# Eleven of the 22 up steps as seven block products, with their weight sums on GpSimd

## The chip, the cores and the metric

The kernel runs on one core of a Trainium2 chip. The core has five engines that work side by side, each through its own queue in order: TensorE (PE, matrix products; its weight loads are listed as PEld), VectorE (DVE), ScalarE (ACT), GpSimd (POOL) and SyncE (SP), which issues most transfers. Matrix products read SBUF and write PSUM. The metric is the device time of one execution in microseconds (us).

## The reference

One layer of a hybrid backbone over 512 latent tokens of 1024 channels. The change touches its last part alone, a gated feed-forward layer with a convolution of width 3 along the tokens:

```python
def conv_ffn(h, w_up, conv_w, conv_b, w_down):
    u = dwconv_centred(h @ w_up, conv_w, conv_b)
    a, b = u[..., :D_FF], u[..., D_FF:]
    return (jax.nn.silu(a) * b) @ w_down
...
x = x + gt2 * conv_ffn(modulate(x, norm2_g[l], sh2, sc2), w_up[l], ffn_conv_w[l],
                       ffn_conv_b[l], w_down[l])
```

`h` is 512 x 1024, `w_up` 1024 x 5632 (`D_FF` is 2816), `w_down` 2816 x 1024. All numbers are float32.

## The kernel before

**Products.** Each float32 operand is split in two: a high part, cast to the rounded type that PE takes (`S.copy`, L183, on ACT), and a low part, what is left (`V.tensor_tensor`, L184, on DVE). A product is then three matmuls, high by high, high by low and low by high (`gemm`, L238, L239, L241). A weight tile of 128 x 1024 floats is loaded by SP (L177) into one of three buffers `wraw`, and its parts `whi` and `wlo` have two buffers each. `run` issues the load and the split of a weight one key ahead of its use.

**The up projection** is 22 steps, `up_step(t)`. A step makes 128 channels of `a` and 128 of `b` for all 512 tokens: two products of eight blocks of 128 input channels each, 2 x 8 x 3 = 48 matmuls of 512 columns. The input is held as `h2h` and `h2l` (the tiles `mh` and `ml`). From PSUM, `conv` makes one pass on ACT (L2051) and two on DVE (L2052, L2053); ACT applies silu (L2059), and DVE multiplies the halves into `F["x"]` (tile `fx`, L2065). Step 0 is apart: it goes by halves of the tokens as the norm hands them out (`norm2_k`, L2014 to L2021).

**The down projection** (`down_step`, L2302 to L2304) already uses seven block products instead of eight. `f_sums(t)` makes its operand sums from `fx` after each up step: splits into `fs` (L2031 on ACT, L2032 on DVE) and differences (L2040 to L2045).

**Beside the up steps** stand eight of the 32 steps `m_step` of a modulation vector (two passes of DVE over a raw weight, L813), woven among steps 0 to 17; transposes of the residual stream (`x1_turn`, DVE L2113, and four small transfers on SP each); and two `fold`s, chains of transfers that POOL issues (L789 to L793).

**Order.** A scheduler orders each engine's instructions when the program is built, except inside `tc.manual_schedule(engines=...)`, where the named engines take them as written, and for single instructions given to `tc.keep_in_program_order`. An engine then works its queue in that order; a wait at its head holds up all behind it.

## Time and profile before

Three runs took 1214.69, 1215.36 and 1216.09 us. The parts of the profiled execution that matter here:

| what | us |
|---|---|
| median of the runs | 1215.36 |
| the profiled execution's own time | 1215.35 |
| its span, from the first to the last instruction | 1213.6 |
| up steps 1 to 21, from 874.34 to 1102.61 | 228.27 |
| DVE, ACT and POOL busy in these | 163.37, 94.78, 14.14 |
| median from issue to landing of an up weight (512 KB) in that stage | 3.8 |

A group's row names line, engine, operation, the tiles written and read, their shapes and the count, then the total and the mean time (us, ns), then the idle time of the engine just before them and what ended it. A timeline's row starts with the start and the length in us; neighbours of one kind are merged into one row with their count. PE's matmuls overlap, so their rate is read from their starts.

### The profile page before, as it was taken

Reading aid. Unit: us, or ns where it says so; the run is one execution under the profiler, and the core shown is the slowest. Engines: PE = TensorE matmul, PEld = TensorE weight load, DVE = VectorE, ACT = ScalarE, POOL = GpSimd, SP = SyncE. Lnnn points to the kernel's source line nnn. Section 1 sums busy time; section 2 is a strip of 40 time slices with the busy share of each in tenths; the row PEclk is TensorE's granted clock in tenths of the full one; section 3 lists DMA queues with packets and bytes.
Section 4 is the critical chain, followed back from the end, with each engine's and each line's share of the span. In section 5 each row is a group of like instructions: output and inputs, shape, how many; then the busy total and the mean of one; then the engine's idle time right before and its main releaser. Section 6 shows DMA issues by size and latency. Waiting matters only on the chain.

```text
span 1213.6 us, 17847 instructions
## 1 busy us (share of the span) xinstructions
PE 1203.6 (99%) x6429; PEld 1005.6 (83%) x6429; DVE 918.6 (76%) x1476; ACT 684.4 (56%) x1269; POOL 263.8 (22%) x274
## 2 busy tenths in 40 slices
PE   9999999999999999999999999999999999999998
PEld 6798888888878878788787887888988888888886
DVE  4857887888565588788887978677677767668787
ACT  4557887778543467476575664223544343436654
POOL 0000121100102546264382762000200100110021
PEclk9999999999999999999999999999999999999999
DMA  9655889844747737566477668687266634437662
GB/s 367 253 148 185 161 229 271 170 133 139 170 140 240 228 113 199 157 162 192 145 178 264 176 228 265 221 251 242 50 163 148 195 117 138 130 107 226 213 185 97
DMA packets 129417, 224.30 MB, mean 185 GB/s; under 512 B 27336, under 2 KB 70640, under 8 KB 129328
## 3 DMA queue, kind: packets, MB, share of 16 engines
q1 hardware_dynamic: 115248, 195.61, 52.0%
q0 software_dynamic: 13792, 27.27, 10.1%
q8 instruction: 51, 0.84, 0.3%
q14 instruction: 38, 0.31, 0.1%
q10 hardware_dynamic: 288, 0.27, 0.1%
HBM read 196.17 MB, written 45.02 MB: 199 GB/s over the span
## 4 chain that ended last, share of the span: by engine, by line
PE 90%; DMA 3%; DVE 2%; POOL 2%; issue 1%; ACT 1%; SPq 0%; DVEq 0%; POOLq 0%; ACTq 0%
PE acc L241 18%; PE acc L238 18%; PE acc L239 18%; PE score L979 3%; PE po L1028 3%; PE pt L1015 2%; PE mis L582 2%; PE mis L1754 2%; PE mis L1597 2%; PE mis L2304 2%; PE mis L2302 2%; PE mis L2303 2%; DMA xs_d<-xb 1%; PE acc L2304 1%; PE acc L2302 1%
## 5 line engine op out<-in xcount | busy, mean ns | idle before, releaser
L184 DVE TENSOR_TENSOR wlo<-wraw,whi 128x1024 fp32r<-128x1024 f32 (+1 forms) x115 | 148.3, 1289 | 89.2 <-ACT whi L183 88.3
L183 ACT CAST whi<-wraw 128x1024 fp32r<-128x1024 f32 (+1 forms) x115 | 120.2, 1046 | 154.2 <-PE acc L239 103.4
L238 PE MATMUL acc<-hlh,whi 128*128 128x512 f32 x472 | 192.8, 409 | 0.0
L241 PE MATMUL acc<-hlh,wlo 128*128 128x512 f32 x472 | 185.6, 393 | 0.0
L239 PE MATMUL acc<-hll,whi 128*128 128x512 f32 x472 | 185.0, 392 | 0.0
L238 PE MATMUL acc<-mh,whi 128*128 128x512 f32 x368 | 143.3, 389 | 0.0
L239 PE MATMUL acc<-ml,whi 128*128 128x512 f32 x368 | 143.2, 389 | 0.0
L241 PE MATMUL acc<-mh,wlo 128*128 128x512 f32 x368 | 143.2, 389 | 0.0
L241 PEld LDWEIGHTS acc<-hlh,wlo 128*128 128x128 f32 x472 | 88.6, 188 | 19.9 <-issue 0.5
L238 PEld LDWEIGHTS acc<-hlh,whi 128*128 128x128 f32 x472 | 88.8, 188 | 17.6 <-issue 2.8
L239 PEld LDWEIGHTS acc<-hll,whi 128*128 128x128 f32 x472 | 88.9, 188 | 17.4 <-issue 2.2
L238 PEld LDWEIGHTS acc<-mh,whi 128*128 128x128 f32 x368 | 69.1, 188 | 14.4
L241 PEld LDWEIGHTS acc<-mh,wlo 128*128 128x128 f32 x368 | 69.1, 188 | 14.3
L239 PEld LDWEIGHTS acc<-ml,whi 128*128 128x128 f32 x368 | 69.1, 188 | 14.2
L164 POOL DMA_DIRECT2D dsum<-wdn x24 | 25.3, 1118 | 194.3 <-DVE wlo L1112 183.7
L988 DVE CUSTOM_DVE_ANT_0 p<-score,winm,nsink 128x512 f32<-128x512 f32 (+1 forms) x64 | 51.8, 810 | 15.3 <-PE score L979 13.8
L995 ACT ACTIVATE p<-p,mneg 128x512 f32<-128x512 f32 (+1 forms) x64 | 49.7, 777 | 15.4 <-DVE mneg L988 14.9
L813 DVE SCALAR_TENSOR_TENSOR tm<-wraw,csil,tm 128x512 f32<-128x512 f32 x56 | 45.9, 819 | 13.1 <-DMA wraw<-wm 12.4
L1023 DVE TENSOR_TENSOR ptl<-pt,pth 128x512 fp32r<-128x512 f32 x72 | 47.5, 685 | 8.4 <-ACT pth L1019 7.7
L238 PE MATMUL acc<-hch,whi 128*128 128x256 f32 x176 | 53.2, 302 | 0.0
L1112 DVE TENSOR_TENSOR wlo<-wraw,whi 128x1024 fp32r<-128x1024 f32 x30 | 36.7, 1223 | 18.3 <-ACT whi L1109 18.2
L241 PE MATMUL acc<-hch,wlo 128*128 128x256 f32 x176 | 49.8, 283 | 0.0
(458 smaller groups left out, 3054.3 us busy)
## 6 DMA issues: line engine op xcount, KB each, us to landing
wraw<-wup SPq DMA_DIRECT2D x44, 512.0 KB, 4.0
dsum<-wdn POOLq DMA_DIRECT2D x24, 704.0 KB, 8.7
wraw<-wm SPq DMA_DIRECT2D x32, 512.0 KB, 4.1
fb<-cs_d SPq DMA_DIRECT2D x32, 512.0 KB, 7.5
wraw<-wx SPq DMA_DIRECT2D x24, 512.0 KB, 4.1
wm<-wm SPq DMA_DIRECT2D x16, 512.0 KB, 7.9
wraw<-wz SPq DMA_DIRECT2D x16, 512.0 KB, 4.7
far<-us_d SPq DMA_DIRECT2D x32, 256.0 KB, 5.1
```

Of the source, the lines that this page charges most:

```text
L183: F["cast"] = S.copy(hi[:, :n], r[:, :n])
L184: F["sub"] = V.tensor_tensor(lo[:, :n], r[:, :n], raw(hi[:, :n]), ALU.subtract)
L238: T.matmul(ps, wh, xh[:, k0 + k, :], start=a, stop=False)
L239: T.matmul(ps, wh, xl[:, k0 + k, :], start=False, stop=False)
L241: T.matmul(ps, wl, xh[:, k0 + k, :], start=False, stop=b)
L813: V.scalar_tensor_tensor(acc, r[:, u * 512 : u * 512 + 512], sc, acc, ALU.mult, ALU.add)
L988: V.tensor_tensor_reduce(p[:, :w], d["ps"][i][:, o0 : o0 + w], m, op0=ALU.add, op1=ALU.min, scale=1.0, scalar=nsink[:, h : h + 1], accum_o ...
L995: S.activation(p, p, AF.Exp, bias=d["mneg"][:, i : i + 1], scale=-1.0, accum_out=d["den"][:, i : i + 1])
L1023: V.tensor_tensor(d["ptl"][x], d["pt"][x], raw(d["pth"][x]), ALU.subtract)
L1112: sum_step(V.tensor_tensor(d["w"][1], d["r"], raw(d["w"][0]), ALU.subtract), 1 + (4 <= g < 12))
L2302: T.matmul(ps, h, wh, start=st, stop=False, skip_group_check=True)
L2304: T.matmul(ps, h, wl, start=False, stop=en, skip_group_check=True)
```

## The change

Steps 3 to 13 no longer make two whole products. The step's two weight tiles and the input are cut in a 2 x 2 scheme (halves of the input channels, `a` against `b`, halves of the tokens), and seven products of four blocks by 256 columns give what eight would. Weight sums are made by POOL, their casts by ACT and low parts by DVE, all for step t + 1 while PE does step t. The products 7 and 4 of a step run during the next one. The core of it:

```diff
+    def input_sums():
+        r = F["h2"]
+        for e, k in ((G, slice(0, HK, 2)), (V, slice(HK, KT, 2))):
+            tc.keep_in_program_order(e.tensor_tensor(r[:, k, :], raw(h2h[:, k, :]), raw(h2l[:, k, :]), ALU.add))
+        b11, b12, b21, b22 = (r[:, HK * i : HK * i + HK, z] for i in range(2) for z in HALF)
+        for x, y, o in ((b12, b11, b11), (b22, b12, b12), (b22, b11, b22), (b21, b22, b21)):
+            G.tensor_tensor(o, x, y, ALU.subtract)
...
+        if which == 1:
+            G.tensor_tensor(o, wb[:, h[0]], wb[:, h[1]], ALU.add)
+        elif which == 2:
+            G.tensor_tensor(o, B["r1", t], wa[:, h[0]], ALU.subtract)
+        elif which == 3:
+            G.tensor_tensor(o, wa[:, h[0]], wb[:, h[0]], ALU.subtract)
+        else:
+            G.tensor_tensor(o, wa[:, h[1]], B["r2", t], ALU.subtract)
...
+            with tc.manual_schedule(engines=EVERY):
+                if old:
+                    quarter(a, 12)
+                seven(t, 5)
+                if older:
+                    conv_rest("b", b, NFF + b)
+                if new:
+                    seven_sum(n, 1)
+                if old:
+                    conv_first("a", a, a, "tb")
+                kept_half(t, 0, B["y", t])
+                if new:
+                    whole_cast(n)
+                if old:
+                    conv_rest("a", a, a)
+                seven(t, 1)
...
+                seven(t, 3)
...
+                if old:
+                    seven(a, 4)
+                    quarter(a, 21)
+                    conv_first("b", a, NFF + a, "tm")
...
+                seven(t, 6)
...
-            weave([up_step(t) for t in range(18)], msteps[24:]) + [up_step(t) for t in range(18, NFF)],
-            [([], lambda: None)] * 6 + [x1_turn(c) for c in range(8)] + [x1_rows] + [([], lambda: None)] * 6 + [([], row_tiles)],
+            [up_step(t) for t in range(15, 18)],
+            msteps[24:28] + [([], lambda: f_sums(0, 2, True)), ([], lambda: f_sums(2, 4, True))] + msteps[28:] + [x1_rows],
+        )
+        + weave(
+            [up_step(t) for t in range(18, NFF)],
+            [([], lambda p=p: f_sums(p, min(p + 2, DK))) for p in (4, 6, 8, 10)] + [([], row_tiles)],
```

Here `seven(t, j)` is product j of step t on PE, `seven_low` and `whole_low` are DVE's low parts, `seven_cast` and `whole_cast` ACT's casts, `quarter` the adds of partial results from PSUM, `conv_first` and `conv_rest` the convolution, now from SBUF, and `put_up` the product into `fx`, now on POOL. Steps 0 to 2 and 15 to 21 stay as before, and step 14 also makes the last two products of step 13. `f_sums` takes two pairs of steps at once and starts after step 14; for its first two calls POOL takes part of the sums. The modulation's steps 24 to 31 move beside steps 15 to 17.

On DVE, one old step in the middle of the stage (`wlo` and `whi` are parts of a weight, `acc` is PSUM, `ta` and `tc` the two halves after the convolution, `fx` and `fs` belong to the down projection):

```order
L184 TENSOR_TENSOR wlo<-wraw,whi 128x1024
L2052 SCALAR_TENSOR_TENSOR ta<-acc,vec,ta 128x511
L2053 SCALAR_TENSOR_TENSOR ta<-acc,vec,ta 128x511
L184 TENSOR_TENSOR wlo<-wraw,whi 128x1024
L2052 SCALAR_TENSOR_TENSOR tc<-acc,vec,tc 128x511
L2053 SCALAR_TENSOR_TENSOR tc<-acc,vec,tc 128x511
L2065 TENSOR_TENSOR fx_8981<-tb,tc 128x512
L2032 TENSOR_TENSOR fs_8984<-fx_8981,fs_8984 128x256
L2040 TENSOR_TENSOR fx_8981<-fx_8981 128x256
```

The same place in the change, one full step (`sraw` is a weight sum of POOL's, the `ring` tiles hold the parts of sums, `mis` is PSUM like `acc`, `te` a kept product):

```order
L2225 SCALAR_TENSOR_TENSOR tm<-tc,vec,tm 128x511
L2226 SCALAR_TENSOR_TENSOR tm<-tc,vec,tm 128x511
L2225 SCALAR_TENSOR_TENSOR tb<-ta,vec,tb 128x511
L2226 SCALAR_TENSOR_TENSOR tb<-ta,vec,tb 128x511
L2172 TENSOR_TENSOR wlo<-wraw,whi 128x1024
L2215 TENSOR_TENSOR tc<-te,acc 128x256
L2164 TENSOR_TENSOR ringe<-sraw,ringrbc_9381 128x512
L2164 TENSOR_TENSOR ringa<-sraw,ringa 128x512
L2208 TENSOR_TENSOR ta<-te,mis 128x256
L2164 TENSOR_TENSOR ringa<-wraw,ringa 128x512
L2164 TENSOR_TENSOR ringb<-sraw,ringb 128x512
L2212 TENSOR_TENSOR ta<-acc,ta 128x256
```

A fifth low part of 512 (L2164) follows as the next row. The convolution's passes read SBUF twice, where before one input was in PSUM; one low part of 1024 has become five of 512; the product into `fx` has left for POOL.

On POOL, what stood between the norm's last piece (L2019) and the down projection before was a chain of transfers:

```order
L2019 TENSOR_TENSOR ml<-ta,mh 128x256 x5
L789 DMA fold_765<-tm 128x512
L791 DMA fold_765<-fold_765 256x128
L791 DMA fold_765<-fold_765 128x128
L791 DMA fold_765<-fold_765 64x128
```

In the change, every full step has this on POOL:

```order
L2151 TENSOR_TENSOR sraw<-wraw 128x512
L2155 TENSOR_TENSOR sraw<-wraw 128x512
L2153 TENSOR_TENSOR sraw<-sraw,wraw 128x512
L2157 TENSOR_TENSOR sraw<-wraw,sraw 128x512
L2232 TENSOR_TENSOR fx_8982<-tb,tm 128x512
```

Four weight sums and the product into `fx` are new there; the chain of transfers now comes behind all of them.

On DVE, steps 15 and 16 before:

```order
L184 TENSOR_TENSOR wlo<-wraw,whi 128x1024
L2052 SCALAR_TENSOR_TENSOR tc<-acc,vec,tc 128x511
L2053 SCALAR_TENSOR_TENSOR tc<-acc,vec,tc 128x511
L2065 TENSOR_TENSOR fx_8982<-tb,tc 128x512
L2043 SCALAR_TENSOR_TENSOR fx_8981<-fx_8981,fx_8982 128x256
L2044 TENSOR_TENSOR fx_8981<-fx_8982,fx_8981 128x256
L2045 SCALAR_TENSOR_TENSOR ft<-fx_8981,fx_8982 128x256
L813 SCALAR_TENSOR_TENSOR tm<-wraw,csil,tm 128x512 x2
L184 TENSOR_TENSOR wlo<-wraw,whi 128x1024
```

and in the change, between two weights of steps 15 and 16:

```order
L184 TENSOR_TENSOR wlo<-wraw,whi 128x1024
L2067 SCALAR_TENSOR_TENSOR tc<-acc,vec,tc 128x511
L813 SCALAR_TENSOR_TENSOR tm<-wraw,csil,tm 128x512
L2068 SCALAR_TENSOR_TENSOR tc<-acc,vec,tc 128x511
L813 SCALAR_TENSOR_TENSOR tm<-wraw,csil,tm 128x512
L2080 TENSOR_TENSOR fx_8981<-tb,tc 128x512
L813 SCALAR_TENSOR_TENSOR tm<-wraw,csil,tm 128x512
L2067 SCALAR_TENSOR_TENSOR ta<-acc,vec,ta 128x511
L813 SCALAR_TENSOR_TENSOR tm<-wraw,csil,tm 128x512
L2068 SCALAR_TENSOR_TENSOR ta<-acc,vec,ta 128x511
L184 TENSOR_TENSOR wlo<-wraw,whi 128x1024
```

The passes of the modulation (L813) now come four between two weights.

## The prediction

> **What bounds the kernel now.** The page's first part and its chain come first: TensorE (PE) is busy nearly all the span and holds nine tenths of the chain that ended last, so time can only be won by less work on PE and is lost wherever PE is made to wait.

> ```profile
> PE 1203.6 (99%) x6429; PEld 1005.6 (83%) x6429; DVE 918.6 (76%) x1476; ACT 684.4 (56%) x1269; POOL 263.8 (22%) x274
> PE 90%; DMA 3%; DVE 2%; POOL 2%; issue 1%; ACT 1%; SPq 0%; DVEq 0%; POOLq 0%; ACTq 0%
> ```

> Then the stage that is changed, by a window from the end of up step 0 to the first matmul of the down projection. It holds 21 up steps.

> ```profile
> 874.34:1102.61 228.27, 228.27 (x1010) 188.97 (x1009) 163.37 (x237) 94.78 (x130) 14.14 (x18) 1.00 0.48 137
> ```

> The columns are the window, its length, and the busy time of PE, PEld, DVE, ACT and POOL. PE never waits here; a step takes 228.27/21 = 10.87 us, 0.2265 us for each of its 48 matmuls of 512 columns. DVE is busy 7.8 us of a step, POOL almost never.

> **The matmuls that go.** A step by seven products has 7 x 4 x 3 = 84 matmuls of 256 columns. Such matmuls run just ahead of this stage, in the output projection; these are the 2nd and the 33rd of a row without a break:

> ```profile
> 847.74 0.28 PE L1935 MATMUL acc<-ml,wlast 128*128 128x256 f32 x1
> ...
> 851.45 0.28 PE L1936 MATMUL acc<-mh,wlast 128*128 128x256 f32 x1
> ```

> (851.45 - 847.74)/31 = 0.1197 us each, so seven products take 10.05 us and one product 1.436. Eleven steps save 11 x 0.82 = **9.0 us on PE**, if the other engines keep up.

> **What a step asks of the other engines.** Prices from the groups of 860 to 1115 us:

> ```profile
> L184 DVE TENSOR_TENSOR wlo<-wraw,whi 128x1024 fp32r<-128x1024 f32 x44 | 53.9, 1224 | 55.4 <-ACT whi L183 54.7 <-DMA x_d<-te 0.7
> L184 DVE TENSOR_TENSOR wlo<-dnraw,whi 128x512 fp32r<-128x512 f32 x1 | 0.7, 684 | 0.0
> L2053 DVE SCALAR_TENSOR_TENSOR ta<-acc,vec,ta 128x511 f32<-128x511 f32 x22 | 16.4, 746 | 0.5
> L2032 DVE TENSOR_TENSOR fs<-fx,fs 128x256 fp32r<-128x256 f32 x22 | 9.2, 419 | 4.2 <-ACT fs L2031 4.2
> L813 DVE SCALAR_TENSOR_TENSOR tm<-wraw,csil,tm 128x512 f32<-128x512 f32 x14 | 10.5, 750 | 1.4 <-DMA wraw<-wm 1.2
> L183 ACT CAST whi<-wraw 128x1024 fp32r<-128x1024 f32 x44 | 46.3, 1054 | 56.6 <-PE acc L239 53.6 <-DMA wraw<-wdn 2.7
> L183 ACT CAST whi<-dnraw 128x512 fp32r<-128x512 f32 x1 | 0.6, 617 | 0.0
> L2059 ACT ACTIVATE tb<-ta 128x512 f32<-128x512 f32 x22 | 13.9, 632 | 48.9 <-DVE ta L2053 44.5 <-DVE g2c L2138 2.2 <-DVE g2c L2137 2.2
> L2031 ACT CAST fs<-fx 128x256 fp32r<-128x256 f32 x22 | 8.9, 404 | 30.7 <-DVE fx L2065 29.3 <-DVE fx L2040 1.4
> ```

> ACT has one cast of 1024, five of 512, three passes of 512 and four of 256: 1.05 + 3.09 + 1.90 + 1.62 = 7.7 us, under 10.05. DVE has, by the rows of its order in the change, one low part of 1024, five of 512, four passes of the convolution and three adds of 256 that read PSUM. Back to back each costs 0.08 less than its duration, as the last DVE row of the next fence shows (two instructions of 0.68 in 1.28). So 1.14 + 5 x 0.60 + 4 x 0.66 = **6.8 us with both inputs in SBUF**, and 3 x 0.34 = 1.0 us with one of them in PSUM: 7.8 together. That too would fit beside 10.05, as would POOL by itself with five elementwise instructions of 1.29 (6.5 us). The raw buffer's loop fits as well: from the release of a weight by the low part of product 4 through the load (3.8 us), ACT's cast and DVE's next six instructions back to the same point I count 3.8 + 1.05 + 1.22 + 2 x 0.42 + 3 x 0.68 = 9.0.

> ```profile
> wraw<-wup SPq DMA_DIRECT2D x39, 512.0 KB, 3.8
> ```

> **What does not fit is DVE and POOL together.** In this stage POOL now idles, so the price of running both has to be read earlier, where the scan keeps both busy. The timeline of DVE, then that of POOL, from 694 us:

> ```profile
> 694.59 1.50 DVE L813 SCALAR_TENSOR_TENSOR tm<-wraw,csil,tm 128x512 f32<-128x512 f32 x1
> 696.01 1.26 DVE L1974 TENSOR_SCALAR g1h<-mod 128x8 f32<-128x8 f32 x1
> 697.19 3.42 DVE L184 TENSOR_TENSOR wlo<-wraw,whi 128x1024 fp32r<-128x1024 f32 x2
> 700.53 1.28 DVE L1756 TENSOR_TENSOR te<-mis,far 128x512 f32<-128x512 f32 x2
> ```

> ```profile
> 695.50 1.75 POOL L1574 TENSOR_TENSOR E<-E,dg 128x512 f32<-128x512 f32 x1
> 697.20 2.32 POOL L1571 TENSOR_TENSOR ssq<-ssq,sq 128x512 f32<-128x512 f32 x1
> 699.49 2.26 POOL L1574 TENSOR_TENSOR zs<-y,zs 128x512 f32<-128x512 f32 x1
> ...
> 711.37 1.29 POOL L1574 TENSOR_TENSOR zs<-y,zs 128x512 f32<-128x512 f32 x1
> 712.74 1.30 POOL L1574 TENSOR_TENSOR y<-te 128x512 f32<-128x512 f32 x1
> 714.00 1.30 POOL L1571 TENSOR_TENSOR ssq<-ssq,sq 128x512 f32<-128x512 f32 x1
> ```

> POOL's 128x512 instruction takes 1.29 alone, but 2.32 and 2.26 here. Two low parts of DVE and these two ran one after the other, wlo, ssq, wlo, zs, and filled 697.19 to 701.75, 4.56 us; DVE's two cost 2 x 1.14 alone, so each POOL instruction took (4.56 - 2.28)/2 = **1.14 us in which DVE could not work**. The scalar_tensor_tensor at 694.59 took 1.50 for the 0.75 of its row above. The adds from PSUM at 700.53 kept their 0.68 beside the running zs. So what excludes POOL is a DVE instruction with both inputs in SBUF, and the change gives both engines little else.

> [...]

> A full step thus needs 6.8 + 5 x 1.14 = **12.5 us** of turns at the shared input, more than PE's 10.05 and more than the 10.87 of now. If nothing of DVE's PSUM adds falls under POOL it needs 13.5. The order is written out and in it many waits cross: a low part waits for ACT's cast and the cast for POOL's sum, and behind that low part in DVE's queue stand the adds of 256 that hand PE its bank back for the products 7 and 4. So I take the middle, **13.0**.

> **The sum.** Steps 3 to 14 take 12 x 10.87 = 130.4 us now.
> Steps 5 to 12 are full: 8 x 13.0 = 104.0 (100.0 to 108.0).
> Step 4 lacks two convolution passes (1.32) and the product to fx (1.14): 10.5 (10.0 to 11.0).
> Step 3 has five products (7.2 on PE), but prepares step 4, 4.1 of DVE and 4.6 of POOL, while POOL also makes two low parts of 1024. From the 256-element row below and 1.29 for 512, POOL needs 2.15 ns an element, so 2.39 us for 1024, 2.24 of them exclusive. In all 13.2, part of it early: 11.0 (9.0 to 13.2).
> Step 13 prepares nothing: 10.05. Step 14 is an old step with two products left over: 10.87 + 2.87 = 13.75.
> Together 149.3, **+18.9**.

> ```profile
> L2019 POOL TENSOR_TENSOR ml<-ta,mh 128x256 fp32r<-128x256 f32 x8 | 5.9, 738 | 11.8 <-ACT ta L2018 11.8
> L1574 POOL TENSOR_TENSOR dg<-ident,coef 128x512 f32<-128x512 f32 x24 | 24.9, 1061 | 0.9
> ```

> Ahead of step 3, POOL makes five input sums of 1024 (11.2 exclusive) and four of the first weight's (4.6). DVE adds, beside its usual three low parts and two products (4.6), an input sum, two input low parts and all low parts of step 3 (7.6). That is 28.0 us of turns over two steps of 21.7, some begun early and some needed late. DVE's first low part of step 3 also stands ahead of the low part of step 2's second weight and waits for POOL's fourth instruction. I take +4 (0 to 7).
> In steps 15 to 17 DVE has six low parts (6.8), twelve convolution passes (7.9), three products (1.8), sixteen passes of the modulation that were spread over 18 steps (10.2) and two operand sums (5.0): 31.7 of 32.6 us. POOL's four in the sums add up to 4.6 of waiting. Work is handed on to the light steps 18 to 21; the weights' low parts stand among it. I take +3 (0 to 7).
> The transposes, moved later, are one-input work of 0.7 us and stay hidden under these waits; their DMAs are behind the weight loads on SP as before. Nothing in the down projection is shortened or lengthened.

> 18.9 + 4 + 3 = +25.9. The profiled execution took 1215.35 us, its span 1213.6 and 1.75 around it; it lies on the median of the runs (1215.36). **1215.35 + 25.9 = 1241 us.** By the bounds, steps 3 to 14 take 142.8 to 156.0, so +12.4 to +39.6: 1228 to 1255.

> **The rivals.**
> *PE stays the bound* (faster). The engines' turns could mesh so that POOL works only while DVE waits or reads PSUM. For it: the sums are made a step ahead, and each engine alone fits in 10.05. Against it: the 12.5 is a sum of turns, which no order shortens. Steps 3 to 14 would take 11 x 10.05 + 10.87 = 121.4, -9.0; with +1 at the edges 1207. It decides only if the exclusion does not hold for these tiles. Chance 0.10.
> *Cheap sums.* One POOL group, dg, takes 1.06 with one small factor read over and over. If the sums ran like that, 0.91 exclusive each, a full step needs 11.4. Steps 3 to 14: 8 x 11.4 + 10.05 + 10 + 10.05 + 13.75 = 135, +4.6, and +2 at the edges: 1222. Against it: every row with two full inputs shows 1.29. Chance 0.09, of which 0.02 for within 0.2%.
> *Waits feed one another.* A late low part keeps a raw buffer, the next load starts late, and its 3.8 us no longer lie under other work; DVE's order is fixed, so the delay stays. Two more us in eight full steps and both edges at 7 give 18.9 + 16 + 14 = +48.9: 1264. Chance 0.08.
> The forecast keeps 0.73.

> **How the numbers follow.** The range must hold 8 in 10: the forecast's own 1228 to 1255 and the cheap sums, 1220 to 1256. About 0.2% is what a measurement of this kernel can tell from no change. Faster 0.10, within 0.2% 0.02, slower 0.88.

> **What would show it.** In the changed profile's window of steps 5 to 12, PE should be idle some 3 us a step, released by DVE's low parts; POOL's 128x512 instructions should take about 2 us and DVE's low parts of 512 more than 1 us. If they keep 1.29 and 0.68 and PE is unbroken at 10.05, the forecast is wrong at its root. A window of step 3 and one of steps 15 to 17 show the edges. A wait of PE that ends on a load would speak for the third rival.

## The result: 55.7 us slower, and the profile after

Four runs of the changed kernel took 1267.33 to 1272.94 us, median **1270.82**; four of the kernel before, on the same chip, 1214.69 to 1216.09, median 1215.14. The ratio is 1.0454, with a 95% interval of 1.0429 to 1.0479. The forecast was 1241, its range 1220 to 1256: the direction was right, the size less than half of what came. The profiled execution took 1272.94, 2.1 over the median, so the parts below add up to 57.6 and not to 55.7.

The page of the changed kernel, its busy times, granted clock and chain:

```profile
PE 1214.8 (96%) x6825; PEld 1030.0 (81%) x6825; DVE 984.3 (77%) x1511; ACT 719.9 (57%) x1351; POOL 378.2 (30%) x340
PEclk9999999999999999999999999998889999999999
PE 65%; issue 13%; DVE 11%; DMA 6%; POOL 3%; ACT 1%; SPq 1%; DVEq 0%; POOLq 0%; ACTq 0%
```

PE holds 65% of the chain instead of 90%, and its clock, at 9 in all slices before, drops to 8 in three of them. Where the time lies is shown by windows of the changed kernel, cut at starts of steps on PE: steps 1 and 2, 3 and 4, 5 to 12, 13 and 14, 15 to 21, and the down projection. The columns are the window, its length, the busy time of PE, PEld, DVE, ACT and POOL, PE's clock, the DMA share and GB/s.

```profile
881.32:906.94 25.62, 23.46 (x97) 18.90 (x96) 19.66 (x18) 13.88 (x18) 21.35 (x11) 0.93 0.20 62
906.94:944.27 37.33, 21.31 (x146) 19.89 (x145) 25.57 (x31) 13.47 (x26) 18.34 (x10) 0.82 0.39 99
944.27:1045.49 101.22, 86.39 (x674) 84.15 (x673) 96.88 (x109) 57.78 (x106) 62.08 (x39) 0.97 0.33 97
1045.49:1069.40 23.91, 23.91 (x158) 21.97 (x157) 17.57 (x23) 12.25 (x22) 6.16 (x4) 1.00 0.56 176
1069.40:1160.22 90.82, 79.86 (x339) 63.58 (x337) 70.55 (x97) 32.86 (x44) 19.03 (x22) 0.98 0.48 142
1160.22:1271.20 110.98, 105.09 (x473) 87.24 (x471) 89.26 (x108) 65.73 (x90) 13.16 (x11) 0.99 0.58 187
```

Before, a step took 10.87 and the down projection 1213.6 - 1102.61 = 110.99, as now. So all of it comes ahead of the down projection, 7.0 us of the first row already in step 0 (step 1 starts at 881.32 instead of 874.34):

| part | before | after | difference | forecast |
|---|---|---|---|---|
| to the start of step 3 | 896.08 | 906.94 | +10.9 | +4 |
| steps 3 and 4 | 21.7 | 37.3 | +15.6 | -0.2 |
| steps 5 to 12 | 87.0 | 101.2 | +14.3 | +17.0 |
| steps 13 and 14 | 21.7 | 23.9 | +2.2 | +2.1 |
| steps 15 to 21 | 76.1 | 90.8 | +14.7 | +3 |
| sum | | | +57.6 | +25.9 |

Steps 5 to 14 came out near the forecast. The two edges, given 7 us, cost 25.6, and steps 3 and 4, given nothing, cost 15.6.

The waits of PE from 850 us on in the changed kernel (who waited for whom: us in all, times, the longest):

```profile
PE acc L2195 <- DVE tc L2215: 13.9, 9, 2.3
PE acc L241 <- DVE wlo L184: 11.6, 6, 4.6
PE mis L2195 <- ACT te L2202: 11.5, 4, 9.1
PE acc L2093 <- POOL ml L2019: 2.8, 1, 2.8
```

In the kernel before, PE waits for nothing there. The first row is step 4 and the full steps: PE waits for the add of 256 that hands it a bank back. The second lies in steps 2 and 15 to 19, the third with 9.1 us in step 3, the fourth in step 0, ahead of everything the forecast looked at.

### The profile page after: what moved, and what is told of

It is laid out like the page before. It is cut to its first block, busy times and chain, and to the rows that moved or that the text cites. A ratio compares the mean times of both kernels' runs of the same rounds, so it can differ in the third digit from the quotient of the medians.

```text
span 1271.2 us, 18887 instructions
## 1 busy us (share of the span) xinstructions
PE 1214.8 (96%) x6825; PEld 1030.0 (81%) x6825; DVE 984.3 (77%) x1511; ACT 719.9 (57%) x1351; POOL 378.2 (30%) x340
## 4 chain that ended last, share of the span: by engine, by line
PE 65%; issue 13%; DVE 11%; DMA 6%; POOL 3%; ACT 1%; SPq 1%; DVEq 0%; POOLq 0%; ACTq 0%
PE acc L241 9%; PE acc L238 9%; PE acc L239 9%; PE score L979 3%; PE po L1028 3%; PE pt L1015 2%; PE mis L582 2%; DMA fold<-fold 2%; PE mis L1754 2%; PE mis L1597 2%; DMA xs_d<-xb 2%; PE mis L2533 2%; PE mis L2532 2%; PE mis L2531 2%; PE acc L2533 1%
## 5 line engine op out<-in xcount | busy, mean ns | idle before, releaser
L239 PE MATMUL acc<-hll,whi 128*128 128x512 f32 x472 | 185.1, 392 | 0.0
L183 ACT CAST whi<-wraw 128x1024 fp32r<-128x1024 f32 (+1 forms) x93 | 96.9, 1043 | 115.1 <-PE acc L239 58.6
L184 DVE TENSOR_TENSOR wlo<-wraw,whi 128x1024 fp32r<-128x1024 f32 (+1 forms) x93 | 122.7, 1319 | 44.2 <-ACT whi L183 41.4
L241 PEld LDWEIGHTS acc<-hlh,wlo 128*128 128x128 f32 x472 | 88.6, 188 | 20.0 <-issue 0.5
L239 PEld LDWEIGHTS acc<-hll,whi 128*128 128x128 f32 x472 | 88.9, 188 | 17.5 <-issue 2.2
L241 PE MATMUL acc<-mh,wlo 128*128 128x512 f32 x192 | 76.6, 399 | 11.6 <-DVE wlo L184 11.6
L238 PE MATMUL acc<-mh,whi 128*128 128x512 f32 x192 | 76.3, 397 | 1.5 <-ACT whi L183 1.5
L239 PE MATMUL acc<-ml,whi 128*128 128x512 f32 x192 | 76.3, 397 | 0.0
L988 DVE CUSTOM_DVE_ANT_0 p<-score,winm,nsink 128x512 f32<-128x512 f32 (+1 forms) x64 | 51.9, 810 | 15.4 <-PE score L979 13.9
L995 ACT ACTIVATE p<-p,mneg 128x512 f32<-128x512 f32 (+1 forms) x64 | 49.7, 777 | 15.4 <-DVE mneg L988 14.8
L813 DVE SCALAR_TENSOR_TENSOR tm<-wraw,csil,tm 128x512 f32<-128x512 f32 x56 | 47.1, 841 | 13.4 <-DMA wraw<-wm 12.9
L241 PEld LDWEIGHTS acc<-mh,wlo 128*128 128x128 f32 x192 | 36.9, 192 | 21.8 <-DVE wlo L184 14.1
L239 PE MATMUL acc<-hcl,whi 128*128 128x256 f32 x176 | 49.7, 282 | 0.0
L1719 ACT ACTIVATE E<-fb,TX 128x128 f32<-128x128 f32 x128 | 44.6, 389 | 8.5 <-DMA fb<-cs_d 4.7
## 6 DMA issues: line engine op xcount, KB each, us to landing
wraw<-wup SPq DMA_DIRECT2D x44, 512.0 KB, 3.6
wraw<-wm SPq DMA_DIRECT2D x32, 512.0 KB, 4.5
fb<-cs_d SPq DMA_DIRECT2D x32, 512.0 KB, 7.0
wraw<-wx SPq DMA_DIRECT2D x24, 512.0 KB, 4.4
wm<-wm SPq DMA_DIRECT2D x16, 512.0 KB, 8.3
wraw<-wz SPq DMA_DIRECT2D x16, 512.0 KB, 5.1
```

The source lines that it names most:

```text
L183: F["cast"] = S.copy(hi[:, :n], r[:, :n])
L184: F["sub"] = V.tensor_tensor(lo[:, :n], r[:, :n], raw(hi[:, :n]), ALU.subtract)
L238: T.matmul(ps, wh, xh[:, k0 + k, :], start=a, stop=False)
L239: T.matmul(ps, wh, xl[:, k0 + k, :], start=False, stop=False)
L241: T.matmul(ps, wl, xh[:, k0 + k, :], start=False, stop=b)
L813: V.scalar_tensor_tensor(acc, r[:, u * 512 : u * 512 + 512], sc, acc, ALU.mult, ALU.add)
```

## The experiments

The table holds the profiled runs, in us: how much later than before step 5 starts (before: 917.82), steps 5 to 12 (before 87.0), steps 15 to 21 (before 76.1); and the median and the ratio with its interval. The middle columns are of one execution each. The runs of one kernel lie 0.5 to 8.5 us apart, and steps 5 to 12 took 101.2 to 103.6 in the kernels that leave them as in the change, so small differences between rows say little.

| kernel | step 5 | 5 to 12 | 15 to 21 | median | ratio |
|---|---|---|---|---|---|
| the change | +26.5 | 101.2 | 90.8 | 1270.82 | 1.0454 (1.0429-1.0479) |
| sums_out | +14.9 | 88.4 | 91.9 | 1250.55 | 1.0291 (1.0276-1.0306) |
| sums_dve | +23.6 | 101.1 | 90.1 | 1267.31 | 1.0428 (1.0411-1.0446) |
| all_dve | +38.5 | 93.5 | 76.2 | 1263.27 | 1.0396 (1.0381-1.0412) |
| turns_free | +15.2 | 103.7 | 91.6 | 1263.98 | 1.0388 (1.0356-1.0420) |
| turn_tile | +22.5 | 104.9 | 89.1 | 1267.73 | 1.0435 (1.0419-1.0451) |
| turns_first | +20.9 | 103.4 | 90.7 | 1267.24 | 1.0422 (1.0404-1.0440) |
| turns_ta | +14.8 | 102.9 | 88.3 | 1260.80 | 1.0368 (1.0348-1.0388) |
| head_ta | +19.2 | 102.9 | 88.6 | 1263.18 | 1.0390 (1.0373-1.0407) |
| edges | +13.9 | 103.2 | 88.2 | 1259.71 | 1.0365 (1.0350-1.0381) |
| insums_out | +8.5 | 102.7 | 88.0 | 1254.39 | 1.0320 (1.0303-1.0337) |
| nofold | +24.4 | 103.6 | 85.8 | 1268.83 | 1.0444 (1.0426-1.0461) |
| mods_out | +25.3 | 102.4 | 77.6 | 1259.38 | 1.0360 (1.0345-1.0376) |
| fsums_dve | +24.6 | 103.1 | 87.8 | 1270.06 | 1.0449 (1.0434-1.0465) |
| mods_early | +51.6 | 102.5 | 77.6 | 1285.25 | 1.0579 (1.0563-1.0595) |
| free | +36.3 | 83.2 | 77.6 | 1253.20 | 1.0316 (1.0299-1.0333) |
| free3 | +9.8 | 82.6 | 77.7 | 1224.09 | 1.0067 (1.0052-1.0082) |
| free4 | +4.3 | 82.7 | 77.6 | 1220.34 | 1.0036 (1.0023-1.0049) |
| best | +9.9 | 93.0 | 82.9 | 1240.59 | 1.0200 (1.0185-1.0215) |

### Who makes the weight sums

**sums_out** leaves the sums of `seven_sum` out, **sums_dve** makes them on VectorE (the first of four is shown):

```diff
@@ sums_out
-        o = B["r%d" % which, t] = F["c3pool"].tile([P, 512], F32, tag="sraw", name="sraw", bufs=4)
...
+        B["r%d" % which, t] = {1: wb[:, h[0]], 2: wa[:, h[0]], 3: wb[:, h[0]], 4: wa[:, h[1]]}[which]
@@ sums_dve
-            G.tensor_tensor(o, wb[:, h[0]], wb[:, h[1]], ALU.add)
+            V.tensor_tensor(o, wb[:, h[0]], wb[:, h[1]], ALU.add)
...
```

> The four weight sums of each step (128x512, GpSimd) are left out: casts and low parts read the raw weight halves, so the products of sums are of other numbers; everything else is as in the change. Theory A (turns at the shared SBUF input bind the step): a full step then needs 6.8 us of VectorE instructions with two SBUF inputs, 1.0 of its adds from PSUM and 1.14 for the one GpSimd product, 8.9 together, under TensorE's 10.05. Steps 5 to 12 fall from 12.65 to 10.1-10.6 us, -17 to -20 us in all, and TensorE's waits on VectorE's adds (13.9 us) all but vanish; with some help in steps 2 to 4 the total is 1243 to 1254. Rival B (the written order: the adds that hand TensorE its banks back stand behind low parts, and loads come late, whoever makes the sums): steps stay at 11.8 or more, total 1262 to 1272.

> The same four sums are made by VectorE instead of GpSimd, at the same places of the order; nothing is left out. Theory A: a sum costs 0.60 us of VectorE's own time in place of a turn of 1.14, so a full step needs 6.8 + 2.4 + 1.0 + 1.14 (the product into fx, still GpSimd's) = 11.3 us instead of 12.5: steps 5 to 12 gain 8 to 11 us, total 1258 to 1264. Rival B2 (VectorE is simply full: 12.39 of 12.46 us busy in step 5, each instruction truly that long): four more instructions of 0.68 lengthen a step by 2.4, total 1285 to 1292.

Groups of steps 5 to 12 in the changed kernel (the count, then the total and mean time in us and ns, then the idle time before):

```profile
L2226 DVE SCALAR_TENSOR_TENSOR tb<-ta,vec,tb 128x511 f32<-128x511 f32 x8 | 13.3, 1662 | 0.3
L2164 DVE TENSOR_TENSOR ringa<-wraw,ringa 128x512 fp32r<-128x512 f32 x5 | 6.5, 1292 | 0.0
L2215 DVE TENSOR_TENSOR tc<-te,acc 128x256 f32<-128x256 f32 x8 | 3.3, 407 | 0.0
L2232 POOL TENSOR_TENSOR fx<-tb,tm 128x512 f32<-128x512 f32 x8 | 13.9, 1734 | 6.2 <-DVE tm L2226 6.2
```

and of the same steps in sums_out:

```profile
L2156 DVE TENSOR_TENSOR ringa<-wraw,ringa 128x512 fp32r<-128x512 f32 x15 | 10.1, 681 | 0.0
L2218 DVE SCALAR_TENSOR_TENSOR tb<-ta,vec,tb 128x511 f32<-128x511 f32 x8 | 13.3, 1669 | 0.3
```

The window of these steps in sums_out:

```profile
932.68:1021.04 88.36, 82.15 (x674) 80.93 (x673) 75.06 (x108) 58.13 (x106) 13.41 (x8) 1.00 0.38 110
```

Without the sums the low part of 512 is back at 0.68 us, and only the convolution pass that meets the one POOL instruction left (the product into fx) keeps its 1.67. The adds that read PSUM took 0.41 to 0.43 in both. Five of the eight steps take 10.08, so the written order and the loads allow PE's own pace: theory A holds, rival B (11.8 or more) falls. The expected 17 to 20 us were 12.9, because the three steps with a transpose took 12.6 to 12.7; in free4 below, where the transposes have a tile of their own, two of the three are gone. The turn is smaller than I had it: DVE's busy time is 96.88 with 39 POOL instructions and 75.06 with 8, so a sum costs DVE 21.82/31 = 0.70 us, not 1.14.

sums_dve missed its range by 3 us: steps 5 to 12 stay at 101.1. At 0.70 a turn, not 1.14, a sum that costs VectorE 0.60 of its own gains only some 0.1. Rival B2 (15 us a step) is out. The steps with a transpose took 13.4 to 14.6, the others 11.5 to 12.0. **all_dve** takes POOL and the transposes' tile out of the question: sums and the product into fx on VectorE, and the transposes in a tile of their own (modulation moved as in mods_early, odd rows as in head_ta):

```diff
-        G.tensor_tensor(F["x"][t % 2][:, t // 2, :], B["oa", t], B["ob", t], ALU.mult)
+        V.tensor_tensor(F["x"][t % 2][:, t // 2, :], B["oa", t], B["ob", t], ALU.mult)
```

> As the bound, but with the weight sums, all made by VectorE, and the product into fx too, so GpSimd does no elementwise work in steps 4 to 13 (transposes: one buffer); nothing is left out. Theory A: VectorE needs 6.8 + 2.4 + 0.6 + 1.0 = 10.8 us for a full step, no turns are lost, so steps 5 to 12 take 10.8 to 11.3 and the total is 1222 to 1232, better than the change by 40 and no better than the kernel before. Rival L (order): steps stay at 11.8 or more as with the sums alone on VectorE, total 1236 or more.

Windows of all_dve, steps 5 to 12 and 5 to 11:

```profile
956.32:1049.79 93.47, 84.41 (x675) 82.58 (x674) 90.87 (x149) 57.00 (x107) 0.00 (x0) 0.98 0.35 108
956.32:1034.41 78.09, 72.34 (x591) 70.92 (x590) 77.01 (x128) 48.27 (x91) 0.00 (x0) 1.00 0.32 101
```

Seven steps take 78.09/7 = 11.16 us, DVE 11.0 of them busy, POOL none: the count of 10.8 was near. Step 12 took 15.4, 13.9 of them DVE's, which the expectation did not have. The total missed by far, for a reason told under the tail: the modulation steps' new place.

### Step 3: the transposes of the residual stream

In the changed kernel step 3 has one wait of 9.06 us. SyncE's queue, ScalarE and VectorE around it (starts, lengths, and in brackets the idle time before and its releaser):

```profile
907.23 14.92 SPq L2345 DMA_DIRECT2D x_d<-te  x16
922.26 22.23 SPq L177 DMA_DIRECT2D wraw<-wup  x6
```

```profile
906.50 1.29 DVE L2342 STREAM_TRANSPOSE te<-x 128x512 f32<-128x512 f32 x2
917.34 1.30 DVE L2342 STREAM_TRANSPOSE te<-x 128x512 f32<-128x512 f32 x2
927.16 1.38 DVE L2172 TENSOR_TENSOR wlo<-wraw,whi 128x1024 fp32r<-128x1024 f32 x1 [8.52 <-ACT whi L2168]
```

```profile
921.51 0.37 ACT L2202 COPY te<-mis 128x256 f32<-128x256 f32 x1 [6.94 <-DMA x_d<-te]
926.08 1.04 ACT L2168 CAST whi<-wraw 128x1024 fp32r<-128x1024 f32 x1 [4.20 <-DMA wraw<-wup]
```

Three queues interlock. Two of the first four transposes run at 906.50, the other two stand behind the low parts of step 3, at 917.34. SP issues the transfers of the first two, waits for the others, issues theirs, and only then, at 922.26, the next weight load, for which ACT's cast for step 4 waits until 926.08. And ACT cannot copy the kept product to `te` until a transfer has read that buffer, so PE gets its bank at 921.93. In the kernel before, too, such transfers stood between the loads of up weights, but PE did not wait:

```profile
865.42 8.14 SPq L2116 DMA_DIRECT2D x_d<-te  x7
880.67 0.35 SPq L177 DMA_DIRECT2D wraw<-wup  x1
```

Four edits took this apart. **turns_free** lets the scheduler place the transposes, **turn_tile** gives them one buffer of their own, **turns_first** and **turns_ta** write the first four ahead of the output projection's last steps, in `te` and in `ta`:

```diff
@@ turns_free
-            tc.keep_in_program_order(V.transpose(t, x1[c // 4][:, c % 4, :]))
+            V.transpose(t, x1[c // 4][:, c % 4, :])
@@ turn_tile
...
-            t = tmp("te")
+            t = F["c3pool"].tile([P, 512], F32, tag="turn", name="turn", bufs=1)
@@ turns_first and turns_ta
-        + [([], vectors)]
+        + [([], vectors)] + [x1_turn(c) for c in range(4)]
...
-        + [x1_turn(0), x1_turn(1), up_step(2), x1_turn(2), x1_turn(3), seven_in(3)]
+        + [up_step(2), seven_in(3)]
@@ turns_ta
-            t = tmp("te")
+            t = tmp("ta" if c < 4 else "te")
```

> The transposes of the residual stream are no longer held to the place where they are written, so the scheduler may put the first four ahead of step 1, as in the kernel before; the rest is the change. Theory C (step 3's 22.3 us come from them: they stand on VectorE behind all low parts of step 3, their eight transfers of 0.55 us each stand on SyncE ahead of a weight load of step 4, and they hold both buffers te that the kept products need): step 3 falls to 11 to 14 us, -8 to -12 in all, total 1259 to 1263. Rival D (step 3 is late because GpSimd's two input low parts of 1024 end at 912.2 and all casts stand behind them): step 3 stays above 18 us, total 1267 to 1273.

> The transposes of the residual stream keep their place but write a tile of their own, turn (one buffer; the weight sums give up one of their four for it); the kept products have both te buffers to themselves. Theory C1 (the 9.06 us in step 3 are the wait for a te buffer): that wait goes, but a weight load of step 4 may still stand behind the transposes' transfers; steps 3 and 4 fall from 37.3 to 28-32 us, total 1261 to 1266. Theory C2 (it is SyncE's queue: the load of step 4's weight is issued only after the transfers): ScalarE's kept copy in step 3 still stands behind that weight's cast, steps 3 and 4 keep 35 or more, total 1268 to 1272.

> The first four transposes of the residual stream stand ahead of the last steps of the output projection, so that neither their tiles te nor their transfers meet the up steps' weights; the rest is the change. Theory C2 (steps 3 and 4 are late because SyncE's queue holds the weight load of step 4 behind these transfers, which wait for transposes that stand behind all of step 3's low parts): steps 3 and 4 together fall from 37.3 to 22-26 us, step 5 starts at 929 to 934 instead of 944.3, total 1256 to 1261. Rival M (the turns of VectorE and GpSimd ahead of step 4 are a fixed amount and only change their place): step 5 starts after 938, total 1264 to 1271.

> As turns_first, but the first four transposes write the tile ta (three buffers) instead of te. Theory C2 (steps 3 and 4 are late through the transfers ahead of a weight load on SyncE, and the earlier total was spoilt by the wait for te ahead of step 0): that wait of 4.8 us goes, steps 3 and 4 keep about 26.8, step 5 starts at 930 to 935, total 1257 to 1262. Rival M (a fixed amount of turns only changes its place): step 5 starts after 938, total 1264 or more.

turns_free took steps 3 and 4 from 37.3 to 23.6 us (step 3 took 8, so rival D is out), but its new order put a weight's low part behind two input low parts in step 2 (a wait of 4.0 us), and step 3 began later, so the total ended 1 us above its range. turn_tile settled little: with one buffer, the transposes now waited on VectorE for each other's transfers (1.88 and 4.15 us), and steps 3 and 4 stayed at 35.9. turns_first brought these to 26.8, but the transposes' `te` collided ahead of step 0. The wait there:

```profile
PE mis L285 <- ACT te L1948: 4.8, 1, 4.8
```

So by its total it fell under rival M. turns_ta takes away that collision alone: 26.8 again, step 5 at 932.6, 1260.80 us, all inside theory C2, rival M out:

```profile
905.86:932.64 26.78, 20.20 (x146) 18.88 (x145) 25.79 (x27) 13.35 (x26) 17.51 (x10) 0.94 0.32 99
```

The transposes' place is worth 10 us. How much of it was SyncE's queue and how much the buffer is not shown: the rows above have both, and turn_tile did not part them. The other 5 us of steps 3 and 4 (26.8 instead of 21.7) were not taken apart.

### Ahead of step 3

**head_ta** writes the odd rows as before and copies them:

```diff
-            t = F["h2"][:, k, z]
+            t = tmp("ta")[:, :HL]
...
-            G.tensor_tensor(h2l[:, k, z], t, raw(h2h[:, k, z]), ALU.subtract)
+            G.tensor_tensor(h2l[:, k, z], t, raw(h2h[:, k, z]), ALU.subtract); S.copy(F["h2"][:, k, z], t)
```

> The odd rows of the normed input go to the temporary ta again, as in the kernel before, and ScalarE copies them from there to h2raw (eight small copies more); the rest is the change. Theory E (h2raw's first write stands behind the end of the output projection, which gives TensorE a gap of 2.85 us in step 0 and 10 us at half clock): step 0 ends at 874 to 876 instead of 881.3, the clock stays at 1.0 there, and the start of step 3 moves by the same, -5 to -7.5, total 1263 to 1266. Rival F (the input sums on GpSimd set the start of step 3 anyway, and they are no earlier): step 0 ends earlier but step 3 starts within 1.5 us of 906.9, total 1269 to 1273.

Step 1 began at 873.7, 0.6 earlier than in the kernel before, and step 3 at 899.7 instead of 906.9: theory E. In the change these rows went to a new tile, `h2raw`, whose first write came at 862.60, where `ta` had its first at 857.17 before, and step 0 paid a gap of 2.85 us and 10 us of half clock.

**edges** puts head_ta, turns_free and nofold (below) together:

> Three edits at once: the odd rows go to ta again (measured alone: -7.6), the transposes are free (alone: -6.8, with -13 in step 3 and +8 in steps 1 and 2), the folds are replaced. If the three are independent: 1270.8 - 7.6 - 6.8 - 6 = 1250, range 1247 to 1254. If the +8 of the free transposes was made by the late norm, it vanishes with it: 1240 to 1246. If the head has a fixed amount of turns to do between the norm and step 4 (theory A for the head: VectorE and GpSimd alternate there without a pause), what one edit gains the other loses, and it ends at 1254 to 1259. Steps 5 to 12 keep 12.5 us in all three.

It ended 0.7 us above the last of the three cases: gains ahead of step 5 do not add up (12.6 us earlier there, where the three alone gave 11.2, 7.2 and 2.0). **insums_out** shows part of what fills that stretch; it is turns_first with head_ta and without the input sums:

```diff
-            tc.keep_in_program_order(e.tensor_tensor(r[:, k, :], raw(h2h[:, k, :]), raw(h2l[:, k, :]), ALU.add))
...
+        b11, b12, b21, b22 = (raw(h2h[:, HK * i : HK * i + HK, z]) for i in range(2) for z in HALF)
```

> As turns_first, with the odd rows in ta again, and without the input sums (five GpSimd instructions of 1024 and one of VectorE): the four blocks are taken from the high parts as they are, so the products with sums are of other numbers; their casts and low parts stay. Theory A for the head (some 28 us of turns between the norm and step 4, of which the input sums are 12.3): step 5 starts at 914 to 922, total 1242 to 1250. Rival N (the head is late for another reason, such as loads): step 5 starts after 927, total 1253 or more.

Step 5 starts at 926.3, between the two theories, and the total, 4 us above theory A's range, is in rival N's; turns_first's wait ahead of step 0 (5.2 us here) is in it. From the start of step 1 to that of step 5 it takes 6.8 us less than turns_first. The input sums cost about that, not 12.

### Steps 15 to 21

**nofold** makes the last two quarters of the modulation vector on TensorE, **mods_out** leaves the eight steps out, **fsums_dve** takes POOL out of the operand sums, **mods_early** writes the steps earlier:

```diff
@@ nofold
-    FOLDS = {cg: dpool.tile([P, 512], F32, name="fold%d" % cg) for cg in (6, 7)}
+    FOLDS = {}
...
@@ fsums_dve
-        W = G if pool else V
+        W = V
@@ mods_out
...
-            msteps[24:28] + [([], lambda: f_sums(0, 2, True)), ([], lambda: f_sums(2, 4, True))] + msteps[28:] + [x1_rows],
+            [([], lambda: f_sums(0, 2, True)), ([], lambda: f_sums(2, 4, True)), ([], lambda: folded(6))] + [x1_rows],
@@ mods_early
-        + weave([os_step(o) for o in range(3, 8)], msteps[10:18])
-        + weave([out_step(o) for o in range(5)], msteps[18:24])
+        + weave([os_step(o) for o in range(3, 8)], msteps[10:22])
+        + weave([out_step(o) for o in range(5)], msteps[22:32])
...
-            msteps[24:28] + [([], lambda: f_sums(0, 2, True)), ([], lambda: f_sums(2, 4, True))] + msteps[28:] + [x1_rows],
+            [([], lambda: f_sums(0, 2, True)), ([], lambda: f_sums(2, 4, True))] + [x1_rows],
```

> The two last folds of the modulation vector, chains of nine transfers each that GpSimd issues, are replaced by four transposes on TensorE and one reduction on VectorE, as the other quarters of the vector have them. Theory G (step 19's 17.4 us come from VectorE's queue: an addition to mod waits there 8.07 us for the fold's last transfer, a weight's low part stands behind it, and TensorE pays a gap of 4.64 us and some 3 us at half clock): steps 15 to 21 fall from 90.8 to 84-86, total 1264 to 1266. Rival H (VectorE has too much to do in the tail, and the wait only fills time that it would lose anyway): steps 15 to 21 keep 89 or more, total 1269 to 1273.

> The eight modulation steps beside steps 15 to 17 are left out, with their eight loads of 512 KB, sixteen passes of VectorE and both folds; the last quarter of the modulation vector is then its bias alone. Theory H (these passes and loads crowd VectorE and the three raw buffers): steps 15 to 18 fall from 51.6 to 44-47 and step 19 to 11, total 1256 to 1260. Rival I (the operand sums of the down projection, now in six lumps, hold the low parts up): steps 15 to 18 keep 49 or more and only step 19 gets shorter, total 1263 to 1267.

> GpSimd's four instructions in the first two lumps of operand sums go to VectorE; the rest is the change. Theory A (a turn of GpSimd costs VectorE 1.14 us, doing it itself 0.60): steps 15 and 16 fall from 25.0 to 22.5-24.5, total 1268 to 1270.5. Rival J (VectorE is simply full there): 2.4 us more, total 1271.5 to 1274.

> The modulation steps 18 to 31 stand earlier (twelve among the five steps of the attention and scan outputs' last projections, ten among the five of the output projection), so that none stands beside the up steps; nothing is left out. Theory H (the bunched passes cost the tail 13 us): steps 15 to 21 fall from 90.8 to 77-80, and if VectorE has room where they go, total 1256 to 1261. Rival K (the earlier stages have no room for them either): steps 15 to 21 fall, but the start of step 1 is 5 or more us later, total 1263 or more.

VectorE and then TensorE at the longest wait of the tail, in the changed kernel:

```profile
1124.29 0.16 DVE L797 TENSOR_TENSOR mod<-mod,vec 128x4 f32<-128x4 f32 x1 [8.07 <-DMA mod<-fold]
1124.37 0.68 DVE L2062 SCALAR_TENSOR_TENSOR fx<-fx,fx 128x512 f32<-128x512 f32 x1
1124.97 1.22 DVE L184 TENSOR_TENSOR wlo<-wraw,whi 128x1024 fp32r<-128x1024 f32 x1
```

```profile
1126.24 0.50 PE L241 MATMUL acc<-mh,wlo 128*128 128x512 f32 x1 [4.64 <-DVE wlo L184]
```

A 128x4 add waits for the last transfer of a fold, and a weight's low part stands behind it. Without the folds the tail falls by 5.0 us, as theory G had it (the total, 1268.83, is only 2.0 below the change's and missed its range; in its profiled run steps 5 to 12 took 2.4 longer). Without the modulation steps it falls by 13.2 to 77.6, 1.5 above the 76.1 of before: theory H, inside its range. Its window of steps 15 to 21:

```profile
1069.44:1147.06 77.62, 76.67 (x338) 62.67 (x337) 60.93 (x81) 32.57 (x44) 5.11 (x4) 1.00 0.32 99
```

The operand sums are not the cause: mods_out keeps them all. Made by VectorE alone they gave 3.0 us in the tail, and the total is as theory A had it. mods_early shows the same 77.6, but the steps cost more where I put them: step 5 starts 25.1 us later than in the change. Rival K was right on where they went, and free and all_dve carry this cost too.

### What is left of the products, and the best of it

**free**, **free3** and **free4** are bounds; **best** keeps everything. Their edits are those above, joined as the expectations say.

> A bound, not a version: the weight sums are left out (casts and low parts read raw halves, so products of sums are of other numbers), the odd rows go to ta, transposes have a tile of their own (two buffers) at their place, the modulation steps stand early. What is left of the change is its products, its input sums and its order. Theory A: steps 4 to 13 at 10.1 us each without the 12.6 of the steps behind transposes, step 3 at 10 to 13, steps 15 to 21 at 77-80, start of step 3 at 897 to 901: total 1212 to 1220, so even with free weight sums the change would win at most a few tenths of a per cent. Rival L (the written order still holds it back): steps above 10.6, total 1224 or more.

> A bound: as turns_first, with the odd rows in ta, the later four transposes in a tile of their own, the weight sums left out (casts and low parts read raw halves) and the modulation steps 24 to 31 left out. Input sums stay. Theory A: steps 4 to 13 at 10.1, steps 15 to 21 at 77.6, start of step 5 at 917 to 924: total 1210 to 1219. If step 5 starts later than 927, something else than turns and transposes holds the head: 1222 or more.

> The bound free3 without the input sums too, so that no sums are made at all in the up stage but those of the down projection. Theory A: the products save their 11 x 0.79 us; step 5 starts at 913 to 917, total 1206 to 1211, 4 to 9 under the kernel before. Rival O (the written order or the loads eat the saving even without sums): 1214 or more.

> Nothing is left out: transposes as in turns_ta (the later four in a tile of their own), the odd rows in ta, all weight sums, the product into fx and all operand sums on VectorE, the folds replaced by transposes on TensorE. By what the single edits gave: step 1 starts at 872 to 875, step 5 at 921 to 927, steps 5 to 12 take 11.0 to 11.3 each, steps 15 to 21 81 to 85: total 1227 to 1238, the fastest of the kernels that keep the seven products whole, and still 12 or more above the kernel before. If it ends under 1218, VectorE's 10.8 us a step is too high a count.

free's steps came as expected but for steps 12 (12.4 us) and 3 (23.7), its total did not, with mods_early's cost in it. free3 and free4 ended 5 and 9 us above their ranges. free3's step 5, at 927.6, met the sign named for it, that something else than turns and transposes holds the head: turns_first's wait for `te` ahead of step 0 is in both (3.8 and 4.4 us). Windows of free4, steps 3 and 4, 5 to 12, 13 and 14, 15 to 21:

```profile
901.62:922.10 20.48, 18.29 (x145) 17.47 (x144) 16.93 (x24) 12.13 (x24) 1.13 (x1) 1.00 0.24 78
922.10:1004.85 82.75, 81.40 (x675) 80.86 (x673) 74.83 (x108) 58.43 (x105) 13.42 (x8) 1.00 0.43 119
1004.85:1028.76 23.91, 23.91 (x159) 21.97 (x157) 17.61 (x23) 12.31 (x22) 6.16 (x4) 1.00 0.63 198
1028.76:1106.36 77.60, 76.67 (x339) 62.73 (x337) 60.91 (x81) 32.61 (x44) 5.08 (x4) 1.00 0.32 99
```

From step 3 to the down projection free4 takes 204.7 us, against 1102.61 - 896.08 = 206.5 before. Even with the weight and input sums for nothing and no modulation beside it, 1.8 us of the 9.0 are left: steps 3, 4 and 12 lose some 5 to waits, the tail 1.5. Ahead of step 3 it is 5.5 late, with the wait of 4.4 for `te`. So rival O is right on the time, and theory A on the pace: seven of the steps 5 to 12 take 10.08 to 10.20.

best, which computes everything, is the fastest of the kernels that do, at 1240.59, 2.6 above its range and 2.0% above the kernel before. Steps 5 to 12 took 11.6 each, not 11.0 to 11.3, and the wait of 2.8 us in step 0 that head_ta had taken away is back in it; the cause stays open. No version that beats the kernel before was found. free4 is itself 0.4% slower; without what it loses ahead of step 3 it would win 1.8 us. Weight sums added up by transfers long before, as the down projection has them, were not tried.

## Why the prediction was right in the middle and wrong at the edges

- **What bounds the kernel, and the saving on PE.** Right. Unhindered steps take 10.08 (10.05 forecast), step 13 10.1, step 14 13.8 (13.75).
- **VectorE and GpSimd exclude each other.** Right for the instructions shown: the low parts ringa<-wraw of 512 took 1.29 us in the mean with GpSimd's sums beside them and 0.68 without, and the adds from PSUM are not lengthened (0.41 to 0.43 in both). That the engines take turns at a shared input was my estimate; the runs show the longer instructions, not where they wait. The size of a turn was off: 0.70 for a sum, 0.9 for the product into fx (1.67 instead of 0.75), not 1.14, so a step's five turns cost 3.7 us instead of 5.7. Steps 5 to 12 still took 101.2 of the 104 (100 to 108), since DVE also had the adds in full (1.2 a step), three transposes (2.1) and 4.3 us of waiting. That the number came so close is in part luck: these made up for the smaller turns.
- **"The transposes, moved later, are one-input work of 0.7 us and stay hidden under these waits; their DMAs are behind the weight loads on SP as before."** This step failed: it gave the transposes no cost. Their own 0.7 us held (1.29 for the two at 906.50, while a low part of GpSimd's ran). The transfers of the first four stand ahead of the load that step 4's cast waits for, and they hold the buffer that step 3's kept product needs. Nor does "as before" hold, as the two rows of the kernel before show. I priced the instruction and not its place in three queues. It is worth 10.5 of the 15.6 us in steps 3 and 4 (37.3 to 26.8 with the transposes out of the way).
- **Head +4 (0 to 7).** The mechanism given, turns of the input sums and step 2's low part behind step 3's, is there (input sums about 7 us, the wait of 2.2 us in step 2). Missing was step 0: the tile `h2raw` and its gap of 2.85 us, 7.2 us at the start of step 3 by head_ta. Without it step 3 starts 3.7 us late, against the 4 forecast.
- **Tail +3 (0 to 7).** This step failed too, by 11.7 us. I counted DVE's 31.7 of 32.6 us and took it to fit. The modulation steps there cost 13.2 us: 5.0 by the fold at the head of VectorE's queue; the other 8.2, in their passes and loads, were not taken apart. A sum that nearly fills an engine is not a sum that fits.
- **A term that no step had: the clock.** Seven stretches at half clock, told below; their cost is inside the items above.
- **The down projection.** Right: 110.98 against 110.99.
- **The rivals.** PE as the bound fell with PE's waits, cheap sums with the steps of 12.65 us where they wanted 11.4, though their 0.91 a sum was nearer to the 0.70 than the forecast's 1.14. "Waits feed one another" gave 1264, the nearest number, but by another mechanism: PE's waits in the full steps end on VectorE's adds, not on loads, and these steps cost less than forecast, not more.

## What to carry to other kernels

Price a moved step at every queue it enters: what it holds up on the issuing engine, which load stands behind its transfers, and who needs its buffers. Where two engines lengthen each other's instructions, as GpSimd's sums did to VectorE's low parts here (ringa<-wraw 1.29 us, 0.68 without them), compare the turn with the work taken away before moving work from the full engine to the idle one (here a turn was 0.70 us, the work 0.60; steps 5 to 12 took 101.2 with the sums on GpSimd and 101.1 on VectorE). And give each new gap of the bounding engine a second price for the clock (here some 13 us of PE's busy time in seven stretches at half clock, by the estimate below).

## What the runs showed of the hardware

**Half clock behind windows of 3.41 us with 2.1 us or more of idling.** In the changed kernel the granted clock was 0.50 in seven stretches of the up stage, from 863.85, 901.39, 915.05, 928.70, 979.90, 1017.45 and 1126.67 us on; each is one or three times 3.41 us long, and all starts lie on one grid of 3.413 us. Windows of that grid just ahead of four of them, and the two windows over which the gap of step 5 falls:

```profile
860.44:863.85 3.41, 1.30 (x11) 1.10 (x10) 1.61 (x2) 2.59 (x5) 0.67 (x1) 1.00 0.00 0
897.98:901.39 3.41, 1.25 (x6) 1.01 (x6) 3.37 (x3) 1.78 (x3) 3.33 (x3) 1.00 0.07 19
976.49:979.90 3.41, 1.28 (x11) 1.21 (x11) 3.41 (x6) 1.41 (x3) 0.72 (x2) 1.00 0.17 20
1014.04:1017.45 3.41, 1.29 (x11) 1.22 (x11) 3.41 (x6) 1.41 (x3) 0.72 (x2) 1.00 0.21 19
949.18:952.59 3.41, 2.45 (x21) 2.24 (x19) 3.38 (x4) 0.37 (x2) 1.88 (x2) 1.00 0.00 0
952.59:956.00 3.41, 2.25 (x18) 2.25 (x19) 3.41 (x6) 1.57 (x5) 1.62 (x1) 1.00 0.39 101
```

```profile
863.85:874.09 10.24, 9.50 (x44) 9.50 (x45) 4.17 (x11) 3.74 (x9) 3.54 (x5) 0.50 0.21 53
...
sum 37.54, PE 29.04 PEld 26.91 DVE 20.77 ACT 13.81 POOL 14.87; mean PE 4.15 PEld 3.84 DVE 2.97 ACT 1.97 POOL 2.12
```

A matmul of 256 columns took 0.213 us there and 0.120 at full clock (0.427 and 0.227 for 512). So of the 9.50 busy us of the first stretch some 4.2 are loss, more than the gap of 2.85 ahead of it, and of the 29.0 of all seven some 13. Not all of it adds to the time: steps 8 and 11, behind the stretches of steps 7 and 10, took 11.3 where others took 12.5, so there part of it probably lies under the turns.
